# A decoder block on one core: two operand pairs made anew in the second half, rotated blocks stored one product later, and a reordered turn to the last projection

## The chip, the cores and the metric

The kernel runs on one core of a Trainium2 chip. Its engines run side by side, each through its own list of instructions in order: TensorE (PE in the profile; PEld are its weight loads), VectorE (DVE), ScalarE (ACT), GpSimd (POOL) and SyncE (SP). SP issues most of the transfers and ScalarE some stores; the rows SPq and ACTq are those issues. An engine waits on semaphores, for another engine or for a transfer, and whatever stands behind a waiting instruction on its list waits too. The metric is the device time of one execution in microseconds.

## The reference, cut to what matters

One layer of a decoder block on 2048 rows of width 1024, in float32:

```python
mod = silu(c) @ w_mod[l] + b_mod[l]
shift, scale, gate = jnp.split(mod, 3, axis=-1)
h = rms_norm(x, g_norm[l]) * (1.0 + scale[:, None, :]) + shift[:, None, :]
proj = h @ w_in[l]                       # 1024 -> 8 x 1024
x_rnn, z_rnn, q, k, v, z_attn, g_r, g_a = jnp.split(proj, IN_SPLITS, axis=-1)
xc = causal_depthwise_conv(x_rnn, conv_w[l], conv_b[l])
hr = rg_lru(xc, w_a[l], b_a[l], w_x[l], b_x[l], lam[l], positions)
y_rnn = (hr * silu(z_rnn)) @ w_out_rnn[l]
qh = apply_partial_rope(q.reshape(B, S, N_HEADS, HEAD_DIM), cos, sin)   # first 32 of 128 channels
kh = apply_partial_rope(k.reshape(B, S, N_HEADS, HEAD_DIM), cos, sin)
o = dilated_attention_mixture(qh, kh, vh)   # three (window, dilation) groups, merged by softmax weights
y_attn = (o * silu(z_attn)) @ w_out_attn[l]
merged = sigmoid(g_r + bg_r) * y_rnn + sigmoid(g_a + bg_a) * y_attn
x = x + gate[:, None, :] * (merged @ w_o[l])
return rms_norm(x, g_final)
```

## The kernel before

Every float32 product is made of three passes over rounded parts (`mm3`): high by high, high by low, low by high. So each operand is first split: ScalarE writes the rounded high part (`hi_act`, the rows of L160), and POOL or VectorE subtracts it from the raw value to get the low part (`lo_pool`, L166; `lo_dve`, L169).

The program has three stages.

*The input projection* goes over the rows in two halves of 1024 (`f` is 0, then 1). Its weights, apart from those of v, are taken in 28 pairs of column blocks, and each pair is multiplied by Strassen's scheme in Winograd's form (`strassen`): seven products in place of eight, of twelve matmuls each, with the left operands numbered 0 to 6. Three of the seven (0, 4 and 5) are plain blocks of the weight matrix (`PLAIN`), four are sums of blocks. In the first half `operand_events` loads a pair's four raw blocks (a11, a21, a22, a12; tiles R0 to R4), makes the sums s1 and s2 on VectorE, splits the seven operands into tiles S0 to S6 (`split_s`), and stores on ScalarE's queue, to sD, those that the second half will not make again. In the second half `load_next` keeps the ring of seven S tiles full: it loads an operand from sD, or, for the three plain ones of 26 of the pairs, loads the raw block, which `split_next` splits four products ahead. `prod` calls both after each product. Pairs 23 and 25 hold the first 32 channels of q's and k's heads; their results are turned by the rotary tables (`rotated`: shuffle, turn, add, and a store of four parts on SP). Pairs 22, 24, 26 and 27 are other blocks of q and k, which `plain` stores to qT and kT.

Ahead of the pairs of each half stand the products of v (`second_values` for the second half): their sums are copied out by ScalarE (tiles ev, L769) and stored by SP to vN (L771). A table `plan` says after which of their parts (t, i) the first operands of pair 0 are loaded. During the second half, pieces of other work stand at counts of products: the output projections' weights are split and stored to wD (`output_weights`), and the sums of W_o for the last stage, gated per channel, are stored to oD (`gated_weight`, tiles wo, ws).

*Attention and the output projections.* While attention runs head by head, a generator (`steps`) adds, between its products, the two projections `y_rnn` and `y_attn`: 64 tiles, each with eight steps k, with weights loaded from wD into S0 to S3 (`load_w`, `load_wd`), right operands y loaded into R0 to R3 and split (`load_y`, `split_y`; tiles yh and yl), and gates loaded to tiles fg (`load_g`, four buffers). `evict` multiplies a tile by its gate on VectorE, `store` writes it to mrT or meT. The last 16 tiles (two right operands side by side, with weights taken from the raw matrix, tiles rw) run in `output_products`, after attention.

*The last product*, `merged @ w_o`, is again by seven products: its left operands are read from meT (`operands`: raw, sums, split), its right ones F from W_o and oD (`load_o`, `gate_o`, `hi_o`, `lo_o`; tiles or, four buffers). The parts of F are numbered 0 to 27, four to a factor; `at_step` puts their loads and splits at steps of the last 16 tiles, and `late_parts` puts the last four between the last products' operands.

## Time and profile before

| | |
|---|---|
| runs shown, us | 2246.97, 2252.91, 2254.46 (median 2252.91) |
| profiled execution | 2250.71 us, span 2248.6 us |
| mean granted clock of TensorE | 0.987 |
| busy share of the span | PE 97%, PEld 82%, DVE 65%, ACT 57%, POOL 54% |
| instructions | 34354, of them 11358 matmuls |
| moved by DMA | 520.19 MB, 231 GB/s over the span |
| stores of split operands (sD) | 118 of 512 KB, 3.7 us each to landing |
| loads of split operands (sD) | 118 of 512 KB, 4.9 us |

The profile shows one execution. In a row of an engine's time line stand start and duration in microseconds, engine, source line, operation, output<-input tiles and count, and in brackets the idle time before it with what ended it. `PE X L152 <- ACT S L160: 6.8, 2, 4.4` in the table of waits says that TensorE, about to write X at line 152, waited for ScalarE's S of line 160 for 6.8 us in two waits, the longest 4.4. A row of stretches gives the length, each engine's busy time with its instructions in brackets (PE, PEld, DVE, ACT, POOL), the granted clock, the busy share of the 16 DMA engines and their GB/s.

### The profile page before, as it was taken

The numbers are of one execution on the slowest core, as the hardware profiler recorded it, in microseconds if no ns is written. First come the engines' busy times: TensorE is split into PE (matmuls) and PEld (weight loads), VectorE is DVE, ScalarE is ACT, GpSimd is POOL, SyncE is SP. The second block draws the span as 40 slices with busy tenths as digits, with TensorE's granted clock in tenths as the row PEclk, the third lists the DMA queues.
The fourth block names the chain that finished last, engine by engine and source line by source line (L and its number), as shares of the span: only waits on it lengthen the run. The fifth ranks groups of instructions, "written<-read, shape, count | busy, mean of one in ns | idle before, by whom it ended". The sixth has DMA issues, their size and how long they took to land.

```text
span 2248.6 us, 34354 instructions
## 1 busy us (share of the span) xinstructions
PE 2183.3 (97%) x11358; PEld 1847.6 (82%) x11359; DVE 1462.8 (65%) x2451; ACT 1292.7 (57%) x2560; POOL 1216.4 (54%) x903
## 2 busy tenths in 40 slices
PE   8999999999999999999999998999999999999998
PEld 5998887788877988888888887888889898977787
DVE  5578787778557664555545364467677878745776
ACT  3547767778532436766767511577677887632343
POOL 2267677677566344445445212356565656432886
PEclk9999999999999999999999999999999999999899
DMA  8354665565797647878887899989988888788553
GB/s 283 91 171 163 208 208 179 192 223 200 235 274 223 208 139 236 259 237 241 249 255 245 269 306 294 291 271 289 277 274 264 243 259 252 242 267 258 178 169 131
DMA packets 455433, 520.19 MB, mean 231 GB/s; under 512 B 90360, under 2 KB 333268, under 8 KB 454232
## 3 DMA queue, kind: packets, MB, share of 16 engines
q1 hardware_dynamic: 427492, 434.95, 63.9%
q10 hardware_dynamic: 27572, 83.00, 9.8%
q8 instruction: 90, 1.47, 0.3%
q14 instruction: 87, 0.71, 0.1%
q0 software_dynamic: 192, 0.05, 0.0%
HBM read 340.67 MB, written 177.21 MB: 230 GB/s over the span
## 4 chain that ended last, share of the span: by engine, by line
PE 53%; DMA 7%; DVE 3%; issue 2%; ACT 2%; POOL 2%; SPq 1%; ACTq 0%; POOLq 0%; DVEq 0%
PE pj L152 11%; PE X L152 9%; PE V L152 7%; PE W L152 5%; PE Z L152 5%; PE o L152 4%; PE sc L152 4%; PE Y L152 4%; PE pT L1630 1%; DMA R<-yaT 1%; PE pg L152 1%; DMA wo<-in_w_o_dram 1%; PE pT L1643 1%; DMA meT<-fg 1%; DMA oD<-s 1%
## 5 line engine op out<-in xcount | busy, mean ns | idle before, releaser
L166 POOL TENSOR_TENSOR S<-R,S 128x512 fp32r<-128x512 f32 x278 | 409.2, 1477 | 395.5 <-ACT S L160 358.4
L152 PE MATMUL X<-T,S 128*128 128x512 f32 x1344 | 330.7, 395 | 11.9 <-ACT S L160 6.8
L152 PE MATMUL V<-T,S 128*128 128x512 f32 x1344 | 325.8, 391 | 3.9 <-DVE t L468 2.7
L152 PEld LDWEIGHTS X<-T,S 128*128 128x128 f32 x1344 | 255.6, 191 | 69.0 <-ACT S L160 7.4
L152 PEld LDWEIGHTS V<-T,S 128*128 128x128 f32 x1344 | 251.0, 188 | 59.2 <-issue 1.9
L152 PE MATMUL pj<-yh,S 128*128 128x512 f32 x848 | 287.7, 397 | 5.4 <-DMA S<-wD 3.4
L160 ACT ACTIVATE S<-R 128x512 fp32r<-128x512 f32 x278 | 170.7, 622 | 129.7 <-DMA R<-in_w_in_dram 107.7
L166 POOL TENSOR_TENSOR S<-s,S 128x512 fp32r<-128x512 f32 x108 | 165.7, 1535 | 125.1 <-ACT S L160 92.8
L152 PEld LDWEIGHTS pj<-yh,S 128*128 128x128 f32 x848 | 160.9, 190 | 38.5 <-DVE fg L1861 3.8
L1546 ACT ACTIVATE pp<-pp,st 128x256 f32<-128x256 f32 (+3 forms) x256 | 133.4, 523 | 75.7 <-DVE st L1545 75.3
L152 PE MATMUL pj<-yl,S 128*128 128x512 f32 x424 | 167.8, 396 | 2.3 <-DVE yl L169 1.4
L152 PE MATMUL Y<-T,S 128*128 128x512 f32 x672 | 161.5, 389 | 0.0
L152 PE MATMUL W<-T,S 128*128 128x512 f32 x672 | 161.5, 389 | 0.0
L152 PE MATMUL Z<-T,S 128*128 128x512 f32 x672 | 161.5, 389 | 0.0
L152 PEld LDWEIGHTS Z<-T,S 128*128 128x128 f32 x672 | 126.3, 188 | 26.3
L152 PEld LDWEIGHTS W<-T,S 128*128 128x128 f32 x672 | 126.1, 188 | 26.1
L152 PEld LDWEIGHTS Y<-T,S 128*128 128x128 f32 x672 | 126.1, 188 | 26.1
L160 ACT ACTIVATE S<-s 128x512 fp32r<-128x512 f32 x108 | 67.3, 624 | 119.8 <-DVE s L292 47.6
L169 DVE TENSOR_TENSOR ptl<-pT,pth 128x384 fp32r<-128x384 f32 (+1 forms) x160 | 97.8, 628 | 49.2 <-ACT pth L160 47.0
L962 DVE SCALAR_TENSOR_TENSOR xc<-xr,par,xc 128x512 f32<-128x512 f32 x96 | 97.1, 1012 | 49.9 <-ACT xc L956 47.6
L1545 DVE CUSTOM_DVE_ANT_0 pp<-sc,msk 128x256 f32<-128x256 f32 (+3 forms) x256 | 104.2, 449 | 36.5 <-PE sc L152 34.3
L166 POOL TENSOR_TENSOR kq<-kraw,kq 128x512 fp32r<-128x512 f32 (+1 forms) x64 | 101.3, 1594 | 43.0 <-ACT kq L160 33.5
(383 smaller groups left out, 4855.4 us busy)
## 6 DMA issues: line engine op xcount, KB each, us to landing
sD<-S ACTq DMA_DIRECT2D x118, 512.0 KB, 3.7
S<-sD SPq DMA_DIRECT2D x118, 512.0 KB, 4.9
S<-wD SPq DMA_DIRECT2D x100, 512.0 KB, 5.6
R<-in_w_in_dram SPq DMA_DIRECT2D x196, 256.0 KB, 4.2
wD<-s ACTq DMA_DIRECT2D x64, 256.0 KB, 4.7
T<-in_w_mod_dram SPq DMA_DIRECT2D x8, 1024.0 KB, 12.1
vN<-ev SPq DMA_DIRECT2D x64, 128.0 KB, 2.9
zaT<-ev SPq DMA_DIRECT2D x32, 256.0 KB, 2.8
```

The source lines that it names most:

```text
L152: nc.tensor.matmul(o, lhsT=l, rhs=r, start=st, stop=sp, **kw)
L160: nc.scalar.activation(o, i, AF.Copy)
L166: nc.gpsimd.tensor_tensor(o, i, h.bitcast(F32), ALU.subtract)
L169: nc.vector.tensor_tensor(o, i, h.bitcast(F32), ALU.subtract)
L962: nc.vector.scalar_tensor_tensor(xc, xr[:, i : i + CH], cw(i), xc, ALU.mult, ALU.add)
L1545: nc.vector.tensor_tensor_reduce(pdst, s_ps, mask, 1.0, 3e38, ALU.add, ALU.min, m_)
L1546: nc.scalar.activation(pdst, pdst, AF.Exp, bias=m_, scale=-1.0, accum_out=l_)
L1630: nc.tensor.transpose(pt[:, c0 + j * P : c0 + (j + 1) * P], pp[i][:, k * P : (k + 1) * P], ident)
L1643: nc.tensor.transpose(pt[:, c * P : (c + 1) * P], pp[:, half * P : (half + 1) * P], ident)
```

## The change

TensorE's list of instructions is the same before and after. What moves is the work around it:

- Pairs 22 and 27 (`ANEW`) are not stored to sD in the first half. In the second half their seven operands are made again from four raw blocks, by the same `operand_events`. That takes away 8 stores and 8 loads of 512 KB and adds two raw block loads, eight splits, and the pairs' sums on VectorE. The remaining stores of the last pairs are emptied by a rule instead of all at the end.
- `load_next` is called again behind the work that stands after a product (`load_free`), and not while the next operand belongs to an anew pair.
- At the start of the second half, three of the first loads stand at part (6, 3) of the values' plan instead of four at (7, 0).
- `rotated` stores its block one product after the add.
- Output weights stand 4.5 products apart instead of 4.75; the groups of W_o's sums stand at 1, 13, 26 and 35 instead of 1, 10, 19 and 28, and two of the four sums are written over the loaded tile, so that the ws tile is smaller and the extra tile is gone.
- At the turn from the last head's tiles to the last 16 (tile 47, `TURN`), a weight block is loaded ahead of y's parts 5 and 6, and the gates' loads one step later. From there on the gates' loads stand one tile earlier, and every third tile uses a freed pair of yh and yl tiles in place of fg.
- Three of F's last four parts (24 to 26) are loaded into rw tiles at steps 105 to 109 and split at steps 124 to 127; only part 27 stays late.

```diff
@@ -262,9 +262,10 @@
     PLAIN = {0: (0, 0), 4: (0, 1), 5: (1, 1)}
+    ANEW = (22, 27)
     loaders, unsplit = {}, []
...
-    def operand_events(x, pieces):
+    def operand_events(x, pieces, f=0):
@@ -275,13 +276,13 @@
         def split(i, name):
+            if f:
+                assert n_loaded[0] == 7 * x + i
+                n_loaded[0] += 1
             first[7 * x + i] = t = split_s(v[name])
-            if i not in PLAIN or x not in loaders:
+            if x not in ANEW and (i not in PLAIN or x not in loaders):
                 kept.append((7 * x + i, t))
-            if len(kept) > 2:
-                k, t2 = kept.pop(0)
-                nc.scalar.dma_start(sD[k], t2[:].bitcast(F32))
-            while 7 * x + i == 28 * 7 - 1 and kept:
+            while len(kept) > 2 or kept and x >= ANEW[0] and kept[0][0] < 7 * x + i - 1:
                 k, t2 = kept.pop(0)
@@ -340,6 +341,11 @@
+    def load_free():
+        n = n_loaded
+        while n[0] - NS in used and not (n[0] < 28 * 7 and n[0] // 7 in ANEW):
+            load_next()
+
     def split_next(n):
@@ -371,7 +377,7 @@
         def take():
-            if f:
+            if f and x not in ANEW:
                 return (f, *loaded.pop(0))
@@ -385,10 +391,12 @@
                 used.add(i)
-                while n_loaded[0] - NS in used:
-                    load_next()
+                load_free()
                 split_next(i + 4)
             run_late(n_prod[0])
+            if f:
+                load_free()
+                split_next(i + 4)
@@ -457,7 +465,7 @@
             for d, fn in ((1, load), (4, split), (6, store)):
-                after_prod.setdefault(n_prod[0] + 19 * x // 4 + d, []).append(fn)
+                after_prod.setdefault(n_prod[0] + 9 * x // 2 + d, []).append(fn)
@@ -877,7 +885,8 @@
                         plan[t, i].append(lambda n=n, i=i: load_piece(n + 1, i))
-            plan[7, i].append(lambda i=i: [load_next() for _ in range(4 if i == 0 else 1)])
+            plan[7, i].append(load_next)
+        plan[6, 3].append(lambda: [load_next() for _ in range(NS - 4)])
         plan[7, 2].append(lambda: split_next(0))
@@ -1149,12 +1158,14 @@
                     nc.vector.tensor_tensor(t1[:], t1[:], t0[:], ALU.add)
+
+                def store():
                     for hh in range(4):
...
                         nc.sync.dma_start(dstT[r0 : r0 + 32, :, n * P : (n + 1) * P],
-                                          t1[hh * 32 : (hh + 1) * 32, :].rearrange("p (r j) -> p r j", r=4))
-
-                steps_after(n_prod[0], ((wait, shuffle), (wait + 1, turn), (wait + 2, add)))
+                                          v[0][hh * 32 : (hh + 1) * 32, :].rearrange("p (r j) -> p r j", r=4))
+
+                steps_after(n_prod[0], ((wait, shuffle), (wait + 1, turn), (wait + 2, add), (wait + 3, store)))
@@ -1318,25 +1329,24 @@
                 if not i:
-                    v["t"] = T(ep, [P, 3, CH], F32, "ws")
-                    v["t3"] = T(wq, [P, KH, P], F32, "s1", bufs=1)
+                    v["t"] = T(ep, [P, 2, CH], F32, "ws")
                 t = v["t"]
...
                 else:
-                    tt(v["t3"][:].rearrange("p k m -> p (k m)"), b22, b12, ALU.subtract)
-                    tt(t[:, 2, :], b21, t[:, 1, :], ALU.subtract)
+                    tt(b22, b22, b12, ALU.subtract)
+                    tt(b21, b21, t[:, 1, :], ALU.subtract)
...
             def store_sums():
-                nc.scalar.dma_start(oD[k, :, :3, :], v["t"][:])
-                nc.scalar.dma_start(oD[k, :, 3, :], v["t3"][:].rearrange("p k m -> p (k m)"))
+                nc.scalar.dma_start(oD[k, :, :2, :], v["t"][:])
+                nc.scalar.dma_start(oD[k, :, 2:, :], v[1][:])
...
-        for k, i in enumerate((1, 10, 19, 28)):
+        for k, i in enumerate((1, 13, 26, 35)):
             for d, fn in group(k):
@@ -1410,6 +1420,11 @@
             output_weights()
+            for x, (_, pieces) in enumerate(pair_order()):
+                if x in ANEW:
+                    events.extend((28 * 7 + 7 * x + d - LEAD, 15 * x + i, fn)
+                                  for i, (d, fn) in enumerate(operand_events(x, pieces, f)))
+            events.sort(key=lambda e: e[:2])
@@ -1785,7 +1800,8 @@
         tiles += [(LAST_HEAD + (i ^ (m == KT - 1)), m) for m in range(2, KT) for i in range(2)]
-        Y, G = {}, {}
+        Y, G, spare_g = {}, {}, []
+        TURN = KT * LAST_HEAD - 1
@@ -1849,8 +1865,10 @@
             G[t] = []
-            for src in (grT,) if ys is yaT else (gaT, mrT):
-                g = T(fl, [P, CH], F32, "fg", bufs=4)
+            if t == TURN + 3:
+                spare_g.extend(T(fl, [P, CH], F32, tag, bufs=NY) for tag in ("yh", "yl"))
+            for i, src in enumerate((grT,) if ys is yaT else (gaT, mrT)):
+                g = spare_g[i] if t > TURN and (t - TURN) % 3 == 0 else T(fl, [P, CH], F32, "fg", bufs=4)
                 nc.sync.dma_start(g[:], src[at_])
@@ -1875,7 +1893,8 @@
                     if u + 3 < RAW_W - 1:
-                        load_w(u + 3)
+                        if u + 3 == n_w[0]:
+                            load_w(u + 3)
                     elif u == 2 * KT * LAST_HEAD:
@@ -1884,7 +1903,7 @@
                     evict(t - 1, last)
-                if k == 3:
+                if k == (4 if t == TURN else 3) and t < TURN + 3:
                     load_g(t)
@@ -1908,9 +1927,11 @@
                         else:
-                            if k in (1, 2):
-                                load_y(j + 1, k + 4)
-                            if k == 2:
+                            if k == 1:
+                                load_y(j + 1, 5)
+                            if k == 3:
+                                load_w(n_w[0])
+                                load_y(j + 1, 6)
                                 load_y(j + 1, KT - 1)
@@ -1924,6 +1945,8 @@
                         split_y(LAST_HEAD + 1, i - (4 if i < 8 else 6))
+                    if k == KT - 1 and TURN + 2 <= t < len(tiles) - 1:
+                        load_g(t + 1)
                 yield
@@ -1965,41 +1988,49 @@
             part, k = O_PART[B_ORDER[i // KH]], i % KH
-            raw_o[i] = T(fp, [P, CH], F32, "or", bufs=4)
+            if i in range(24, 27):
+                raw_o[i] = T(fp, [P, KH, P], F32, "rw", bufs=3)[:].rearrange("p k m -> p (k m)")
+            else:
+                raw_o[i] = T(fp, [P, CH], F32, "or", bufs=4)[:]
...
         B_ORDER = "B11", "T2", "T3", "T1", "B21", "T4", "B22"
...
             if i >= 20:
-                at_step(101 + i, lambda i=i: hi_o(i))
-                at_step(102 + i, lambda i=i: lo_o(i))
-                if i > 20:
-                    at_step(103 + i, lambda i=i: load_o(i + 3))
+                at_step(100 + i, lambda i=i: hi_o(i))
+                at_step(101 + i, lambda i=i: lo_o(i))
             else:
...
                 at_step(a + 11, lambda i=i: lo_o(i))
+
+        for i in range(24, 27):
+            at_step(57 + 2 * i, lambda i=i: load_o(i))
+            at_step(65 + 2 * i, lambda i=i: gate_o(i))
+            at_step(100 + i, lambda i=i: hi_o(i))
+            at_step(101 + i, lambda i=i: lo_o(i))
+        at_step(123, lambda: load_o(27))
@@ -2052,11 +2083,8 @@
             jobs += [(7 * x + d - LEAD, len(jobs) + i, fn) for i, (d, fn) in enumerate(operands(x))]
-        late_parts = [(0, load_o, 27)]
-        for i in range(24, 28):
-            late_parts += [(d + (i - 24) // 2, fn, i) for d, fn in ((1, gate_o), (2, hi_o), (3, lo_o))]
-        for d, fn, n in late_parts:
-            jobs.append((d, len(jobs), lambda fn=fn, n=n: fn(n)))
+        for d, fn in ((2, gate_o), (3, hi_o), (4, lo_o)):
+            jobs.append((d, len(jobs), lambda fn=fn: fn(27)))
         jobs.sort(key=lambda e: e[:2])
```

ScalarE at the end of the first half (S: split operands, s: sums, sD: the store, u and T: copies out of PSUM). Before:

```order
L160 ACTIVATE S6_1164_6659<-s2_1138_6500 128x512
L283 DMA sD<-S2_1145_6552 128x1024
L286 DMA sD<-S3_1148_6578 128x1024
L286 DMA sD<-S6_1164_6659 128x1024
L401 ACTIVATE u1_1165_6665<-X_1150_6584 128x512
L537 ACTIVATE T_1153_6619<-pg_1159_6644,mod_41_235,gs_42_236 128x512
L160 ACTIVATE S0_1170_6691<-R0_1160_6649 128x512
```

and after:

```order
L160 ACTIVATE S5_1156_6621<-R3_1123_6399 128x512
L160 ACTIVATE S6_1164_6654<-s2_1138_6497 128x512
L409 ACTIVATE u1_1165_6657<-X_1150_6575 128x512
L545 ACTIVATE T_1153_6614<-pg_1159_6639,mod_41_235,gs_42_236 128x512
L160 ACTIVATE S0_1170_6683<-R0_1160_6644 128x512
L545 ACTIVATE T_1153_6614<-pg_1169_6678,mod_41_235,gs_42_236 128x512
```

The stores of pair 27's operands no longer stand between its last split (from s) and the copy u.

SP at the start of the second half (vN: stores of the values, R: raw block of S0, 4 or 5, S: loads of stored operands). Before:

```order
L771 DMA vN<-ev_1325_7802 128x2x128 x2
L771 DMA vN<-ev_1335_7941 128x2x128 x2
L771 DMA vN<-ev_1336_7945 128x2x128 x2
L255 DMA R3_1338_7950<-in_w_in_dram 128x4x128
L327 DMA S1_1339_7952<-sD 128x1024
L327 DMA S2_1340_7954<-sD 128x1024
L327 DMA S3_1341_7956<-sD 128x1024
L255 DMA R4_1343_7983<-in_w_in_dram 128x4x128
L255 DMA R0_1345_8010<-in_w_in_dram 128x4x128
L327 DMA S6_1346_8038<-sD 128x1024
```

and after:

```order
L779 DMA vN<-ev_1325_7794 128x2x128 x2
L255 DMA R3_1333_7899<-in_w_in_dram 128x4x128
L328 DMA S1_1334_7901<-sD 128x1024
L328 DMA S2_1335_7903<-sD 128x1024
L779 DMA vN<-ev_1339_7940 128x2x128 x2
L779 DMA vN<-ev_1340_7944 128x2x128 x2
L328 DMA S3_1341_7948<-sD 128x1024
L255 DMA R4_1343_7975<-in_w_in_dram 128x4x128
L255 DMA R0_1345_8002<-in_w_in_dram 128x4x128
L328 DMA S6_1346_8030<-sD 128x1024
```

The first raw block and two stored operands stand ahead of two double stores.

SP in the last tiles (meT: store of a tile, fg, yh and yl: loads of gates and of the other branch, or and rw: parts of F, R: blocks of the last product's left operand). Before:

```order
L1866 DMA meT<-fg_4034_21264 128x512
L1970 DMA or_4045_21339<-oD 128x512
L2027 DMA R2_4047_21345<-meT 128x4x128
L1854 DMA fg_4048_21356<-gaT 128x512
L1854 DMA fg_4049_21358<-mrT 128x512
L1970 DMA or_4050_21366<-oD 128x512
L2027 DMA R3_4051_21368<-meT 128x4x128
L1866 DMA meT<-fg_4040_21309 128x512
L1970 DMA or_4053_21384<-oD 128x512
```

and after:

```order
L1884 DMA meT<-yh_3961_20846 128x512
L1872 DMA fg_4041_21346<-gaT 128x512
L1872 DMA fg_4042_21348<-mrT 128x512
L1996 DMA or_4043_21351<-oD 128x512
L1999 DMA rw_4045_21357<-in_w_o_dram 128x512
L2058 DMA R2_4046_21359<-meT 128x4x128
L1999 DMA rw_4047_21368<-in_w_o_dram 128x512
L1996 DMA or_4048_21378<-oD 128x512
L1999 DMA rw_4049_21380<-in_w_o_dram 128x512
L2058 DMA R3_4050_21382<-meT 128x4x128
L1884 DMA meT<-fg_4034_21300 128x512
```

The parts of F that came last are loaded between R2 and R3 into rw, and the gates of a tile stand before the blocks R2 and R3 instead of between and behind them.

10 lines of the change are left out of this document (5 added, 5 removed).

## The prediction

> **What bounds the kernel now.** I read the page first, for the busy shares, then the stretches around the waits, then the engines' own rows there. TensorE is busy 97% of the span, so only the rest can be won.
>
> ```profile
> span 2248.6 us, 34354 instructions
> PE 2183.3 (97%) x11358; PEld 1847.6 (82%) x11359; DVE 1462.8 (65%) x2451; ACT 1292.7 (57%) x2560; POOL 1216.4 (54%) x903
> ```
>
> The table of TensorE's waits (total, times, longest) names who ended them:
>
> ```profile
> PE X L152 <- ACT S L160: 6.8, 2, 4.4
> PE X L152 <- POOL S L166: 4.9, 2, 4.2
> PE Z L152 <- ACT S L160: 4.7, 1, 4.7
> PE pg L527 <- DVE t L547: 3.9, 1, 3.9
> PE pj L152 <- DMA S<-wD: 3.4, 1, 3.4
> PE pj L152 <- ACT yh L160: 2.1, 1, 2.1
> PE pj L152 <- DVE yl L169: 1.4, 2, 1.2
> ```
>
> A wait costs more than its length, because the granted clock falls behind it. Seven stretches, from the view by stretch (length, then each engine's busy time, the clock, the DMA share, GB/s), hold the waits that the change can reach; I call them G, A, B, C, D, E, F in order of time:
>
> ```profile
> 710.00:724.00 14.00, 10.08 (x38) 7.92 (x37) 6.12 (x8) 4.78 (x8) 7.69 (x7) 0.76 0.90 279
> 826.00:841.00 15.00, 10.45 (x47) 8.32 (x46) 1.10 (x2) 3.34 (x7) 1.28 (x1) 0.77 0.81 250
> 1352.00:1363.00 11.00, 7.95 (x27) 5.76 (x26) 2.74 (x6) 1.75 (x3) 2.56 (x3) 0.84 1.04 328
> 1399.00:1411.00 12.00, 8.53 (x29) 6.05 (x28) 5.66 (x9) 3.98 (x7) 0.00 (x0) 0.86 1.02 339
> 1981.00:2002.00 21.00, 16.82 (x62) 11.98 (x61) 6.65 (x9) 5.29 (x9) 6.42 (x5) 0.92 0.89 285
> 2073.00:2087.00 14.00, 9.30 (x30) 7.15 (x29) 8.56 (x12) 5.27 (x10) 9.76 (x7) 0.76 0.83 241
> 2095.00:2110.00 15.00, 9.87 (x31) 6.94 (x31) 12.27 (x13) 6.37 (x14) 12.38 (x8) 0.77 0.42 138
> ```
>
> The loss of a stretch is its length less TensorE's busy time, plus one minus the clock, times its length. G: 3.9 + 0.24 x 14 = 7.3 us. A: 4.55 + 3.45 = 8.0. B: 3.05 + 1.76 = 4.8. C: 3.47 + 1.68 = 5.2. D: 4.18 + 1.68 = 5.9. E: 4.7 + 3.36 = 8.1. F: 5.13 + 3.45 = 8.6. Together 47.9 us, the most that the change can bring here; TensorE's own order of instructions is the same in both kernels, so nothing can come from it.
>
> **The change part by part.** G, end of the first half. ScalarE (ACT, ACTq for its DMA issues) holds the copy u1 behind the last two stores of pair 27's operands:
>
> ```profile
> 712.01 4.25 ACTq L286 DMA_DIRECT2D sD<-S  x2
> 716.31 0.60 ACT L401 ACTIVATE u<-X 128x512 f32<-128x512 f32 x1 [5.80 <-DMA sD<-S]
> 717.61 0.81 DVE L547 TENSOR_SCALAR t<-pg,gs,mod 128x512 f32<-128x512 f32 x1
> 711.19 4.83 SPq L474 DMA_DIRECT2D R<-in_w_in_dram  x4
> ```
>
> VectorE makes t only behind u, and TensorE waits 3.9 us for it. Pair 27 is no longer stored, so u1 follows its split at once, 5.8 us sooner. What is late next are the loads issued from 711.19, which the following products split; I leave 1.0 us for them. Gain 6.3 of 7.3.
>
> A, start of the second half. S0 is split from a raw block whose load stands on SP behind eight stores of values, and the last four of those wait for ScalarE's copies at 827:
>
> ```profile
> 811.35 18.21 SPq L771 DMA_DIRECT2D vN<-ev  x8
> 827.46 0.59 ACT L769 ACTIVATE ev<-X 128x512 f32<-128x512 f32 x1
> 829.65 0.46 SPq L255 DMA_DIRECT2D R<-in_w_in_dram  x1
> 833.13 0.63 ACT L160 ACTIVATE S<-R 128x512 fp32r<-128x512 f32 x1 [5.09 <-DMA R<-in_w_in_dram]
> L166 POOL TENSOR_TENSOR S<-R,S 128x512 fp32r<-128x512 f32 x278 | 409.2, 1477 | 395.5 <-ACT S L160 358.4
> ```
>
> Now R, S1 and S2 are issued ahead of the last four stores, with eight earlier ones behind them no more, so R lands while the copies run. The split follows the copy that ends at 828.05: 0.63 us for the high part, 1.48 for the low one on POOL, done at 830.2. Now the high part alone ends at 833.8. The 4.4 us of wait in the table shrink to 0.8 or so, too little to bring the clock down. Gain 7.0 of 8.0. S3, still behind the stores, is due three products later.
>
> B and C, end of the second half. SP runs behind, held by stores that wait for their adds and by two wo loads:
>
> ```profile
> 1345.90 2.52 SPq L1154 DMA_DIRECT2D qT<-t  x4
> 1350.42 1.48 SPq L255 DMA_DIRECT2D R<-in_w_in_dram  x2
> 1356.24 0.63 ACT L160 ACTIVATE S<-R 128x512 fp32r<-128x512 f32 x1 [17.37 <-DMA R<-in_w_in_dram]
> 1351.67 2.88 PE L152 MATMUL Y<-T,S 128*128 128x512 f32 x12
> 1396.04 0.93 SPq L361 DMA_DIRECT2D R<-yaT  x2
> ```
>
> A four-part store takes 2.5 us of SP, 0.63 an issue. Between the previous pair's S0 load and the R issued at 1350.42 stand 24 issues instead of 30, and a rotated block's store comes one product behind its add, so that SP no longer stands still for it. Six issues are 3.8 us: R lands near 1352.4, not 1356.24, its low part is done 2.1 us later, at 1354.5, and the product is due when Y's twelve matmuls from 1351.67 end, at 1354.4. Gain 4.0 of 4.8: 0.1 of wait and what SP's later lateness may put back. In C the R loads of 1396.04 move ahead of kT stores, and pair 27's four 512 KB loads are gone; VectorE's low part (1.2 us of wait above) stays, with the rest of the clock. Gain 3.5 of 5.2.
>
> What pairs 22 and 27 cost instead: seven splits from four raw blocks each, where there were three splits and four loads of stored operands. Eight more splits are 8 x 0.63 = 5 us of ScalarE and 8 x 1.48 = 12 us of POOL, in a part of the program where POOL has room:
>
> ```profile
> 1236.00:1300.00 64.00, 64.00 (x286) 52.95 (x285) 25.86 (x35) 31.38 (x46) 16.83 (x13) 1.00 0.88 286
> 1296.58 2.88 PE L152 MATMUL X<-T,S 128*128 128x512 f32 x12
> 1299.30 2.88 PE L152 MATMUL V<-T,S 128*128 128x512 f32 x12
> ```
>
> POOL is busy 16.8 of 64 us there, and a product takes 2.72 (1296.58 to 1299.30) against POOL's 1.48. If that cover is gone, each of the two pairs starts late as in A, by 8.0 us; between 0 and 16 I take 2, near the end that POOL's row speaks for. The first half loses eight stores of 512 KB on ScalarE's queue, which G shows blocking; I count no gain beyond G. Storing oD's sums from wo itself, and output weights 4.5 instead of 4.75 products apart, move no end of the path: nothing, unless ScalarE's queue blocks as in G (up to 7.3).
>
> D, the turn to the last projection. TensorE waits 3.4 us for a wD block issued late:
>
> ```profile
> 1978.73 0.49 SPq L355 DMA_DIRECT2D S<-wD  x1
> ```
>
> It goes ahead of one R and two fg loads: three issues and a store's, about 2 us of the 3.4. But no byte is saved, the R that it passes now lands behind its 512 KB, and the loads of y's last parts, each waiting for the split before it, bound the same tiles. Ends 0 and 5.9; I take 2.0, nearer the lower, as the DMA share is 0.89.
>
> E and F, the last tiles. With four fg buffers SP waits for a store to land before each pair of loads; VectorE, in order, waits for the loads, and the sums of the first last-stage operand stand behind it. In F it waits the same way for an or load:
>
> ```profile
> 2066.40 0.93 SPq L1854 DMA_DIRECT2D fg<-gaT  x1
> 2072.74 0.69 DVE L1859 TENSOR_TENSOR fg<-pj,fg 128x512 f32<-128x512 f32 x1 [4.62 <-DMA fg<-gaT]
> 2075.01 0.68 DVE L2038 TENSOR_TENSOR s<-R,R 128x512 f32<-128x512 f32 x1
> 2089.35 0.42 SPq L1973 DMA_DIRECT2D or<-in_w_o_dram  x1
> 2096.25 0.69 DVE L1978 TENSOR_TENSOR or<-or,gate_b 128x512 f32<-128x512 f32 x1 [4.97 <-DMA or<-in_w_o_dram]
> ```
>
> Every third tile now uses freed yh and yl buffers, fg is loaded a tile (two products, 5.4 us) ahead, and three of the four last or loads move before the sums, their splits too. 4.6 us of VectorE's wait in E and 5.0 in F are what TensorE waits (4.7 and 4.2). I leave 1.1 and 1.6 us for POOL, whose low parts are next: 7.0 and 7.0.
>
> Sum: 6.3 + 7.0 + 4.0 + 3.5 + 2.0 + 7.0 + 7.0 = 36.8, less 2 is 34.8. The profiled execution took 2250.71 us (2.1 outside the span), 2.2 under the median of 2252.91; 2250.7 - 34.8 + 2.2 = 2218.
>
> [...] A kept wait need not stay as cheap as it is. This one let the clock be, though B's, not longer, halved it:
>
> ```profile
> 633.11 3.04 PE L152 MATMUL X<-T,S 128*128 128x512 f32 x12 [3.52 <-ACT u L401]
> ```
>
> [...]
>
> **Rivals.** First, the tail is bound by its transfers: DMA shares of 0.89 and 0.83 in D and E speak for it, the 0.42 in F against it. Then D, E and F keep their waits: 2250.7 - 20.8 + 2 + 2.2 = 2234.
>
> Second, slower: SP is held by the raw blocks made anew. Pair 22's fourth load needs a buffer that POOL frees only when it has split the first one, and behind it on SP stand the S loads of pairs 23 to 26 and 27's blocks. They are due from 1296.58 on, five products (13.6 us) behind that split; for it speaks that SP already runs late (1350.42 above), against it POOL's room. If the hold passes 13.6 us, five pairs start as A does: 5 x 8.0 = 40 us, more than the 34.8, so 2258.
>
> Third, the change does not do what it says: the waits only pass on to what is late next, as a DMA issue on SP or ScalarE that waits for another transfer (5.8 us in G). For it: every stretch but F has the DMA at 0.8 or more. 2250.
>
> **How the numbers follow.** The sum 0.57; tail bound by transfers 0.20; hold on SP 0.13; passed on 0.10. The likeliest gives 2218, its own range 2204 (all 47.9 won: 2250.7 - 47.9 + 2.2 = 2205) to 2230. The whole range goes to 2248, which leaves out the slower case and part of the third. About 0.3% (6.8 us) is what a measurement can tell from no change: faster 0.79 (sum, tail rival, a fifth of the third), same 0.07, slower 0.14.
>
> **What would show it.** Right: no store of S between the last split and u1 on ScalarE; the R of the second half issued before 825; SP's R of 1350 and 1396 some 4 us sooner; VectorE's waits for fg and or near 2073 and 2096 gone; clock 0.99 and over. Wrong: TensorE waiting for S at pairs 22 to 27 between 1260 and 1400, or for F and S at 2070 to 2110 still.

## The result, and the profile after

The changed kernel takes 2226.69 us (median of 4 runs, 2225.20 to 2229.14) against 2252.19 us for the kernel before beside it (2246.97 to 2254.46, 4 runs): a ratio of 0.9902 with a 95% interval of 0.9888 to 0.9916. 25.5 us were won where 34.8 were forecast; 2226.7 lies inside the whole range and inside the likeliest case's own, 8.7 us above the forecast of 2218.

The page of the changed kernel, its first rows (busy time, share of the span, instructions):

```profile
span 2227.2 us, 34367 instructions
PE 2174.6 (98%) x11359; PEld 1843.2 (83%) x11359; DVE 1480.7 (66%) x2459; ACT 1297.4 (58%) x2568; POOL 1233.6 (55%) x911
```

and six rows of its table of TensorE's waits (total, times, longest):

```profile
PE V L152 <- DVE t L476: 7.5, 5, 3.0
PE pj L152 <- DVE yl L169: 7.2, 1, 7.2
...
PE pj L152 <- ACT yh L160: 2.2, 2, 1.4
...
PE W L152 <- DVE fg L1877: 2.1, 1, 2.1
PE pj L152 <- POOL yl L166: 1.7, 2, 0.9
...
PE Z L152 <- DVE yh L1877: 1.3, 1, 1.3
```

The waits for S of before (6.8, 4.9 and 4.7 us) are gone from the table, all but a few tenths, and so are the 3.9 for t behind u and the 3.4 for wD. In their place stands one wait that before had no counterpart, 7.2 us for yl, and the waits of V for t (a result that VectorE copies out of PSUM with a sum) have grown from 2.7 to 7.5 us.

Since TensorE's instructions are the same ones, each matmul can be set against itself: its start after, less its start before. Where that difference changes, time was won (negative) or lost. The rows are in us, the times those of the trace before; the last column is a second profile of the changed kernel, beside other runs.

| place | times before | forecast | after | after again |
|---|---|---|---|---|
| pair 22's stores, not in the forecast | 629 to 633 | 0 | -3.8 | -3.8 |
| G, end of the first half | 714 to 724 | -6.3 | -6.5 | -6.5 |
| A, start of the second half | 829 to 840 | -7.0 | -7.1 | -7.2 |
| B | 1354 to 1362 | -4.0 | -5.1 | -5.1 |
| behind B, waits for t | 1362 to 1382 | 0 | +3.2 | +1.4 |
| C | 1397 to 1423 | -3.5 | +10.1 | +8.8 |
| D, the turn | 1981 to 2000 | -2.0 | -1.4 | -1.5 |
| E | 2075 to 2089 | -7.0 | -2.1 | -2.9 |
| F | 2089 to 2110 | -7.0 | -8.2 | -8.1 |
| sum | | -36.8 | -20.9 | -24.9 |

The 2 us that the forecast takes off for the start of the two pairs have no row of their own. The two spans differ by 21.4 us (2248.6 less 2227.2), so the first column of measured numbers accounts for them. Other places, among them 381, 400, 1474, move by up to 1.8 us to either side and not alike in every profile; I read nothing into them.

The same in the view by stretch of the changed kernel (length, busy time of PE, PEld, DVE, ACT, POOL, the clock, the DMA share, GB/s), at the times at which it now does that work, as it runs up to 25 us ahead: G and A, then what became of C, D, and E:

```profile
704.00:713.00 9.00, 9.00 (x47) 7.44 (x46) 5.79 (x9) 5.46 (x10) 7.26 (x6) 1.00 0.84 240
814.00:823.00 9.00, 8.73 (x52) 7.49 (x51) 1.29 (x2) 3.32 (x6) 1.29 (x1) 1.00 0.52 142
...
1375.00:1411.00 36.00, 24.05 (x91) 17.78 (x89) 14.46 (x24) 9.14 (x16) 5.82 (x6) 0.86 0.98 331
1972.00:1990.00 18.00, 15.21 (x55) 10.82 (x53) 6.02 (x8) 5.68 (x9) 6.58 (x5) 0.91 0.94 310
2056.00:2076.00 20.00, 16.59 (x66) 12.95 (x65) 17.68 (x19) 8.21 (x15) 13.05 (x8) 0.91 0.84 236
```

The first has no gap left, the second one of 0.27 us, and both have the full clock: nearly all that could be won there is won. The 36 us of the third hold 12 us of idle TensorE, and there the forecast failed.

**What happens in C.** Row by row, from the time line of the changed kernel (start, duration, engine, line, operation, and in brackets the idle time before it and what ended it):

```profile
1355.82 0.68 DVE L1339 TENSOR_TENSOR wo<-wo,wo 128x512 f32<-128x512 f32 x1
1356.42 0.69 DVE L1340 TENSOR_TENSOR wo<-wo,ws 128x512 f32<-128x512 f32 x1
...
1358.25 0.68 DVE L301 TENSOR_TENSOR R<-R,R 128x512 f32<-128x512 f32 x1
...
1358.98 0.93 SPq L255 DMA_DIRECT2D R<-in_w_in_dram  x2
...
1359.96 6.37 SPq L1165 DMA_DIRECT2D kT<-t  x8
...
1366.43 3.95 SPq L1195 DMA_DIRECT2D kT<-t  x4
...
1370.71 0.83 SPq L1325 DMA_DIRECT2D wo<-in_w_o_dram  x2
...
1375.60 1.23 DVE L1328 TENSOR_TENSOR wo<-wo,gb 128x1024 f32<-128x1024 f32 x1 [7.54 <-DMA wo<-in_w_o_dram]
...
1379.22 4.36 PE L152 MATMUL V<-T,S 128*128 128x512 f32 x12 [3.02 <-DVE t L476]
...
1381.85 0.33 ACTq L1344 DMA_DIRECT2D oD<-wo  x1
...
1382.26 1.69 SPq L367 DMA_DIRECT2D R<-yaT  x2
...
1391.16 0.63 ACT L160 ACTIVATE yh<-R 128x512 fp32r<-128x512 f32 x1 [6.88 <-DMA oD<-wo]
1391.32 1.29 DVE L169 TENSOR_TENSOR yl<-R,yh 128x512 fp32r<-128x512 f32 x2 [7.01 <-DMA oD<-wo]
...
1392.06 0.79 PE L152 MATMUL pj<-yl,S 128*128 128x512 f32 x1 [7.23 <-DVE yl L169]
```

and the two longest of SP's waits between 1335 and 1400:

```profile
SPq L255 <- DVE R L301: 11.5, 1, 11.5
SPq L1195 <- DMA T<-yaT: 4.3, 1, 4.3
```

The 11.5 us are SP standing before pair 27's fourth raw block: its buffer comes free only when VectorE's difference at L301 has read the first one, and that one follows the sums of W_o's third group (L1339, L1340). Behind the hold SP issues twelve kT stores, and only then the two wo loads of the last group, at 1370.71. VectorE sits 7.54 us for them, with the sum t that TensorE waits for behind them (3.02). The group's store to oD is issued at 1381.85. The rows at 1391.16 and 1391.32 show the next stage's splits waiting until that store has landed, 9.3 us after its issue; that yh and yl lie in the memory of wo and ws is read from the built kernel's addresses. TensorE waits 7.23 us. So the last group, which now stands at 35 instead of 28, ends inside the turn to the next stage, and SP's hold makes it later still. The last R loads from yaT do move ahead of two kT stores, as the forecast's step on C has it, but they are issued 7.9 us later than before against TensorE's matmuls (at 1382.26 here, 1396.04 before, in a kernel that was 21.7 us ahead until this place).

**Behind B.** The same queue of VectorE explains the 3.2 us lost right behind B. From 1342.56, when W_o's third group gets its load (5.78 us of wait for it), VectorE works almost without a pause until 1362.9: that group's gating and sums, the rotated block, and pair 27's own sums (L292, L293, L301, 0.7 us each). TensorE waits 0.63 and 2.09 us for a t that stands among them. This is read from the rows; no run varies it alone. The first row and the longer wait:

```profile
1342.56 1.40 DVE L1328 TENSOR_TENSOR wo<-wo,gb 128x1024 f32<-128x1024 f32 x1 [5.78 <-DMA wo<-in_w_o_dram]
...
1359.58 3.01 PE L152 MATMUL V<-T,S 128*128 128x512 f32 x12 [2.09 <-DVE t L476]
```

### The profile page after: what moved, and what is told of

Read it like the earlier page. It is cut to its first block, busy times and chain, and to the rows that moved or that the text cites. A ratio compares the mean times of both kernels' runs of the same rounds, so it can differ in the third digit from the quotient of the medians.

```text
span 2227.2 us, 34367 instructions
## 1 busy us (share of the span) xinstructions
PE 2174.6 (98%) x11359; PEld 1843.2 (83%) x11359; DVE 1480.7 (66%) x2459; ACT 1297.4 (58%) x2568; POOL 1233.6 (55%) x911
## 4 chain that ended last, share of the span: by engine, by line
PE 53%; DMA 6%; DVE 5%; issue 3%; ACT 2%; SPq 2%; POOL 2%; ACTq 0%; DVEq 0%; POOLq 0%
PE pj L152 10%; PE X L152 9%; PE V L152 8%; PE W L152 6%; PE Z L152 6%; PE Y L152 4%; PE o L152 4%; PE sc L152 4%; DMA R<-in_w_in_dram 1%; PE pT L1645 1%; PE pg L152 1%; DMA R<-oT 1%; PE pT L1658 1%; POOL kq L166 1%; DMA kT<-t 1%
## 5 line engine op out<-in xcount | busy, mean ns | idle before, releaser
L166 POOL TENSOR_TENSOR S<-R,S 128x512 fp32r<-128x512 f32 x280 | 414.6, 1486 | 364.6 <-ACT S L160 324.8
L152 PE MATMUL X<-T,S 128*128 128x512 f32 x1344 | 323.6, 389 | 0.3 <-POOL S L166 0.3
L166 POOL TENSOR_TENSOR S<-s,S 128x512 fp32r<-128x512 f32 x114 | 174.0, 1526 | 124.7 <-ACT S L160 80.5
```

Of the source, the lines that this page charges most:

```text
L152: nc.tensor.matmul(o, lhsT=l, rhs=r, start=st, stop=sp, **kw)
L166: nc.gpsimd.tensor_tensor(o, i, h.bitcast(F32), ALU.subtract)
```

## The experiments

Each edit is made to the changed kernel. Medians stand beside the kernel before on the same chip; the comparisons by place are with the changed kernel's first trace unless another is named, positive for time lost.

**W_o's groups where they were.**

```diff
-        for k, i in enumerate((1, 13, 26, 35)):
+        for k, i in enumerate((1, 10, 19, 28)):
```

> The changed kernel with one thing undone: the four groups of W_o's sums stand at 1, 10, 19 and 28 again, not at 1, 13, 26 and 35. Theory L (the late last group is the cause of the 10.0 us lost between 1376 and 1411): its wo loads, VectorE's gating and the store of oD, on whose memory the projection's first yh and yl wait, come early again; the waits of 3.0 and 7.2 us go, and the time falls from 2226.7 by 9 to 12, to about 2216. Theory H (SP held for 11.5 us by pair 27's fourth raw block is the cause): the kT stores and what stands behind them stay late; it falls by under 4, to 2223 or more.

2223.16 us against 2245.11; ratio 0.9906 (0.9889 to 0.9922), no different from the changed kernel's. 1345 to 1411 gets 3.9 us shorter than in the changed kernel's first trace and 0.8 than in its second. The wait of 7.2 us for yl is gone, as theory L has it, but not the 9 to 12 us that it promised: what remains are three waits for yh (6.4 us), and the hold on SP is still 8.8.

**The fourth raw block of an anew pair two products later.**

```diff
-        yield -1, lambda: raw("a12", 0, 1)
+        if not f:
+            yield -1, lambda: raw("a12", 0, 1)
...
+        if f:
+            yield 1, lambda: raw("a12", 0, 1)
```

> The changed kernel, with the fourth raw block (a12) of the two pairs made anew in the second half loaded two products later, behind the split of a11 that frees its buffer. The groups of W_o stay at 1, 13, 26 and 35. Theory H: SP no longer stands still for 11.5 us at pair 27 and 5.4 at pair 22, the last wo load goes out some 8 us sooner, and the waits at 1376 and 1384 fall by 8 or more: about 2218. Theory L: the last group still stands at the end and the store of oD still lands late; under 4 us are won, 2223 or more. If a12 now comes too late for its own split, a new wait of up to 5 us at pair 27's fifth operand takes it back.

2227.31 us against 2245.11; ratio 0.9916 (0.9902 to 0.9931). Only 1345 to 1360 gets shorter, by 1.3 us; against the second trace even that is gone. The edit shortens SP's hold at pair 27 from 11.5 to 7.3 us and does not remove it. With the last group still at 35, TensorE waits 5.9 us for yl, whose split again ends its wait with the landing of the oD store, and 8.0 us for yh, whose split waits for T from yaT. A shorter hold alone is worth nothing that a run can tell.

**Both together.** The two edits above in one kernel.

> Both at once: groups of W_o at 1, 10, 19 and 28, and a12 of the anew pairs two products later. If L and H each carry a part, this is faster than either alone: 2213 or so. If L carries all, it equals the run with the old groups within 2 us; if H carries all, it equals the run with a12 later.

2220.32 us against 2245.11; ratio 0.9887 (0.9872 to 0.9901). That is 2.8 and 7.0 us below the two runs before it, which ran beside it, and the four executions of each do not overlap; the 2213 expected if each cause carries a part is not reached. Against the changed kernel's first trace 1345 to 1411 gets about 9 us shorter, against its second about 6, more than the two alone (3.9 and 1.1, or 0.8 and a loss). The longest of SP's waits of this kernel between 1315 and 1400, then TensorE's from 1330 to 1420:

```profile
SPq L255 <- DVE R L302: 4.8, 1, 4.8
```

```profile
PE V L152 <- ACT S L160: 1.9, 1, 1.9
PE pj L152 <- ACT yh L160: 1.6, 1, 1.6
PE pj L152 <- DVE yl L169: 1.4, 2, 1.2
PE V L152 <- DVE t L479: 0.7, 1, 0.7
```

One profile alone swings by some us here, so I set all of them side by side: from 1362 to 1425, in the times of before, the seven profiles that make both pairs anew and leave both edits out lose 9.2 to 13.3 us against before; the old groups alone lose 9.4, the later block alone 11.8; the three kernels with both lose 4.2, 6.0 and 7.6. So neither edit alone shows a gain outside the swing, and both together do: each cause hides behind the other. Yet against the kernel before, B and C together come out at -1.0 us (-5.1 and +4.1), not at the -7.5 of the forecast. The rest, some 6 us, is five short waits and the clock (0.95 on average from 1340 to 1405 of the kernel with both edits). No run takes apart whether writing two sums over wo, the wider spacing of the output weights, or the anew pair's own splits hold them. That stays open.

**Only pair 27 made anew; pair 22 stored again.**

```diff
-    ANEW = (22, 27)
+    ANEW = (27,)
```

> Only pair 27 is made anew; pair 22's operands are stored in the first half and loaded in the second, as before. Theory S (the 3.5 us wait at 629, which the prediction did not count, went because pair 22's four stores of 512 KB no longer stand in the transfers at 590 to 612): the wait for u at 629 comes back, 3 to 5 us, while the gain at 714 (6.5 us) stays, as that comes from pair 27. Rival: the wait at 629 hangs on which transfer happens to share a semaphore with a store, and is gone or back whatever pair 22 does; it stays away here. In the second half SP's wait at pair 22 (5.4 us) goes, which costs TensorE nothing now, so nothing is won by it.

2227.96 us in one run, against 2245.11. G stays won, with pair 27 still not stored; no run stores pair 27 again, so G's cause rests on the rows. The wait near 630, which the changed kernel no longer has, is back: 4.0 us long, and 5.8 us are lost at that place. ScalarE there, in this kernel and then in the changed one (`sD<-S`: a store of an operand; u: the copy out of PSUM that TensorE needs):

```profile
630.36 0.33 ACTq L287 DMA_DIRECT2D sD<-S  x1
630.73 0.60 ACT L409 ACTIVATE u<-X 128x512 f32<-128x512 f32 x1 [5.11 <-DMA R<-in_w_in_dram]
```

```profile
627.45 0.33 ACTq L287 DMA_DIRECT2D sD<-S  x1
627.83 0.60 ACT L409 ACTIVATE u<-X 128x512 f32<-128x512 f32 x1 [4.64 <-DMA R<-in_w_in_dram]
```

The hold on ScalarE's queue is there in both (5.11 and 4.64 us; 5.26 before), and ends when a raw block lands. What pair 22's missing stores do is let that block's load go out earlier, and u comes 4.7 us sooner against TensorE's matmuls (2.9 by the rows, in a kernel that is 1.8 us behind there). The four 512 KB stores of pair 22 stood at 599 to 612 before. That the loss comes back with them is shown, though the edit also moves the point from which the remaining stores are emptied by the rule; that they act through SP's issue of R is read from the trace and was not varied.

**The plan at the start of the second half as it was.**

```diff
-            plan[7, i].append(load_next)
-        plan[6, 3].append(lambda: [load_next() for _ in range(NS - 4)])
+            plan[7, i].append(lambda i=i: [load_next() for _ in range(4 if i == 0 else 1)])
```

> The changed kernel with the start of the second half as before: the first four operands of pair 0 are loaded at part (7, 0) of the values' plan, behind the last two double stores of v. If the order on SP is what won 7.1 us there, the wait of 4.4 us at pair 0's first product and the half clock behind it come back: 6.5 to 8 us lost there, nothing elsewhere. Rival: the win came from stores or transfers of the first half that are gone; then it stays won, and under 2 us change.

2232.77 us in one run; the kernel before, run once beside this one and the next three, took 2243.30. A loses 8.6 us, a little more than the 6.5 to 8 expected, and the wait that ends it is S's again:

```profile
PE X L152 <- ACT S L160: 5.9, 1, 5.9
```

A is this edit alone, and its whole gain.

**The turn's loads as they were** (no weight block ahead of y's parts, the gates a step earlier).

```diff
-                if k == (4 if t == TURN else 3) and t < TURN + 3:
+                if k == 3 and t < TURN + 3:
...
-                            if k == 1:
-                                load_y(j + 1, 5)
-                            if k == 3:
-                                load_w(n_w[0])
-                                load_y(j + 1, 6)
+                            if k in (1, 2):
+                                load_y(j + 1, k + 4)
+                            if k == 2:
                                 load_y(j + 1, KT - 1)
```

> The changed kernel with the turn to the last projection as before (y's parts 5 and 6 ahead of the third weight block, gates one step earlier). The turn won 1.4 us of the 7.4 lost there. If the order only passes the wait from the weight block to y's part 5 and F's parts, bound by transfers, this run loses 0 to 3 us there, and the wait for the weight block (3.4 us) is back in place of the waits for yl and F. If instead the new order is what costs the remaining 6, this run is no slower at all.

2226.86 us in one run. D loses 1.9 us, against a gain there of 0.5 to 2.0 in the profiles that keep the edit. TensorE's waits from 1960 to 2000, in this kernel and in the changed one:

```profile
PE pj L152 <- DMA S<-wD: 3.7, 1, 3.7
```

```profile
PE pj L152 <- ACT yh L160: 1.4, 1, 1.4
PE pj L152 <- POOL yl L166: 0.9, 1, 0.9
```

The change swaps one wait of 3.7 us for two, 2.3 us in all, as the step on D had it: the weight block passes y's parts, and these are late next.

**The gates' loads and their tiles as before the change** (four fg buffers, loads within the tile).

```diff
-            if t == TURN + 3:
-                spare_g.extend(T(fl, [P, CH], F32, tag, bufs=NY) for tag in ("yh", "yl"))
...
-                g = spare_g[i] if t > TURN and (t - TURN) % 3 == 0 else T(fl, [P, CH], F32, "fg", bufs=4)
+                g = T(fl, [P, CH], F32, "fg", bufs=4)
...
-                if k == (4 if t == TURN else 3) and t < TURN + 3:
+                if k == (4 if t == TURN else 3):
...
-                    if k == KT - 1 and TURN + 2 <= t < len(tiles) - 1:
-                        load_g(t + 1)
```

> The changed kernel with the gates' loads of the last 16 tiles as before: four fg buffers alone, loaded in the tile itself; F's parts 24 to 26 stay early in rw. E (about 2075 before) won about 4 us. If the gates' loads held it, SP waits again for stores to land, and E loses 4 us or more, up to the 7.6 of before, as parts 24 to 26 now stand in the same queue. Rival: F's early parts won E; then this run changes by under 1.5 us.

2231.34 us in one run; 2064 to 2076 loses 2.8 us, between the two expectations. One wait of 5.1 us for S stands where the changed kernel has 1.3 and 2.1. How far this can be read: in the kernel with only pair 27 anew, where nothing is edited in the tail, the same place is 2.3 us shorter than in the changed kernel's first profile. The loss stands outside the swing all the same: E wins 1.4 to 4.4 us against before in every profile that leaves the tail as changed, and loses 0.8 here.

**F's last parts as before the change** (parts 24 to 27 loaded into or tiles after the sums).

```diff
-            if i in range(24, 27):
-                raw_o[i] = T(fp, [P, KH, P], F32, "rw", bufs=3)[:].rearrange("p k m -> p (k m)")
...
-        for i in range(24, 27):
-            at_step(57 + 2 * i, lambda i=i: load_o(i))
-            at_step(65 + 2 * i, lambda i=i: gate_o(i))
...
+        late_parts = [(0, load_o, 27)]
+        for i in range(24, 28):
+            late_parts += [(d + (i - 24) // 2, fn, i) for d, fn in ((1, gate_o), (2, hi_o), (3, lo_o))]
```

> The changed kernel with F's parts 24 to 27 as before, loaded and gated late into or buffers; gates' loads stay early. F (about 2100 before, 8.2 us lost) comes back if the late or load held VectorE there: 6 to 8 us lost at the first product of the second operand. E gets better by up to 3 us, since VectorE's gates of 24 to 26 (5.4 us of wait for the rw load at 2051 after) no longer stand ahead of the tile's evict. Rival: with the gates' loads early the queue is short enough that the or load comes in time; under 2 us lost.

2224.52 us in one run. F loses 6.5 us, as the forecast's step on F says, but E wins 5.6, so that it stands 7.6 us better than before the change: net, this edit is worth 1 us. Here are the same two stretches without it, the second with the loss in it:

```profile
2050.00:2066.00 16.00, 16.00 (x72) 13.24 (x72) 12.94 (x13) 6.66 (x12) 11.54 (x8) 1.00 0.96 304
2066.00:2090.00 24.00, 19.69 (x79) 15.04 (x78) 18.93 (x24) 10.81 (x22) 20.49 (x14) 0.93 0.48 160
```

With the edit TensorE loses time in the first stretch instead. VectorE, in the changed kernel:

```profile
2056.61 0.69 DVE L2004 TENSOR_TENSOR rw<-rw,gate_b 128x512 f32<-128x512 f32 x1 [5.39 <-DMA rw<-in_w_o_dram]
2058.19 0.69 DVE L2004 TENSOR_TENSOR rw<-rw,gate_b 128x512 f32<-128x512 f32 x1 [0.89 <-DMA rw<-in_w_o_dram]
2058.80 0.68 DVE L1877 TENSOR_TENSOR fg<-pj,fg 128x512 f32<-128x512 f32 x1
...
2066.40 1.78 DVE L169 TENSOR_TENSOR F<-or,F 128x512 fp32r<-128x512 f32 x1
2068.11 1.76 DVE L169 TENSOR_TENSOR F<-rw,F 128x512 fp32r<-128x512 f32 x1
2069.79 0.68 DVE L1877 TENSOR_TENSOR fg<-W,fg 128x512 f32<-128x512 f32 x1
```

The part's gate product waits 5.39 us for its load, with an output tile's eviction and the operand's sums behind it, and the part's split stands ahead of the eviction for which TensorE waits 2.1 us. Two readings were left: the wait for the load does the harm, or VectorE has too much to do in these 20 us (17.68 busy, in the view by stretch above). The next runs tell them apart.

**The changed kernel again**, beside the next three runs.

> The changed kernel again, beside the other three. Every theory: the ratio to the kernel before stays near 0.990 (0.9888 to 0.9916 was the interval), and the same places lose as in its first trace: 8 to 12 us at 1360 to 1411 against the first promise of a gain, 3 to 5 us in the tail at 2063 to 2076.

2224.69 us against 2246.24; ratio 0.9897 (0.9874 to 0.9920). The places are in the table at the top: C is lost again, B is won again, and the loss behind B varies by some 2 us from one profile to the next.

**The two edits of C, and the three gate products behind the sums.**

```diff
-            at_step(65 + 2 * i, lambda i=i: gate_o(i))
+            at_step(97 + i, lambda i=i: gate_o(i))
```

> The groups of W_o's sums at 1, 10, 19, 28, pair 27's and 22's fourth block two products later, and the gate products of F's parts 24 to 26 placed behind the sums of the first last-stage operand instead of ahead of an output tile's eviction. Theory T (what is left of the loss in the tail is VectorE's eviction standing behind a gate product that waits 5.4 us for its load): TensorE's waits of 1.3 and 2.1 us at 2063 to 2071 and the halved clock behind them go, 3 to 5.5 us, and the parts of F, still loaded early, keep what was won at 2083 to 2110; with 9 to 10 us at 1345 to 1411 it ends 12 to 15 us below the changed kernel, ratio 0.984 to 0.986. Rival (VectorE is simply full there, 12 of 14 us, and the three gate products only change places with the splits): under 1.5 us in the tail, 9 to 11 below in all, ratio 0.9865 to 0.989.

2219.73 us against 2246.24; ratio 0.9874 (0.9846 to 0.9903), 5 us below the changed kernel beside it, with intervals that overlap and executions that do not (2217.18 to 2222.26, 2222.88 to 2225.81). Theory T wanted 12 to 15, its rival 9 to 11. The gain is C's; in the tail nothing is won (1.1 us lost against the changed kernel's second trace). No gate product waits for its load any more, the sums start 3.8 us sooner (2048.03 after 2060.73, in a kernel that is 8.9 us ahead there), and TensorE waits as long as it did. Its waits from 2040 to 2110:

```profile
PE W L152 <- DVE fg L1880: 2.5, 1, 2.5
PE Z L152 <- ACT F L160: 1.2, 1, 1.2
```

3.7 us, after 3.4. So theory T is wrong: the wait for the load goes, and the loss stays. The rival is what is left. VectorE is busy 19.75 us from 2048 to 2068 here, and its work has only changed places; that its fullness is the bound is argued from this, not varied.

**The same, two steps later still.**

```diff
-            at_step(65 + 2 * i, lambda i=i: gate_o(i))
+            at_step(99 + i, lambda i=i: gate_o(i))
```

> As the one before, with the three gate products two steps later still, so that the second and third stand behind the next eviction (yh from Z). Theory T: no difference of more than 1 us either way, since that eviction has to wait for Z's product anyway. Rival (full VectorE): each gate product of 0.7 us that stands ahead of an eviction costs its own length, so this one is 1 to 2 us faster than the one before.

2221.20 us against 2246.24; ratio 0.9882 (0.9860 to 0.9904). One wait, of 3.9 us, takes the place of the two. The eviction of Z's tile is freed, the next one pays for it: the sum is the same. The gain of 1 to 2 us that the rival expected of this run did not come, so its price of an eviction's delay is not borne out.

**The rotated blocks stored with the add again.**

```diff
-                steps_after(n_prod[0], ((wait, shuffle), (wait + 1, turn), (wait + 2, add), (wait + 3, store)))
+                steps_after(n_prod[0], ((wait, shuffle), (wait + 1, turn), (wait + 2, add), (wait + 2, store)))
```

> The changed kernel, with the rotated blocks stored right behind their add again. By the prediction's step on B the later store is what lets SP go on: SP's raw block loads at 1335 to 1357 come 2 to 4 us later, and TensorE loses 1 to 4 us at 1340 to 1411. Rival (SP is held there by pair 27's fourth block, which waits for its buffer, and the store's place decides nothing): under 1 us in TensorE's offset at 1340 to 1411, and the total within 2 us of the changed kernel.

2224.08 us in one run, 0.6 below the changed kernel's median beside it; its span is 0.1 us shorter than that of the second profile of the changed kernel. Between 1340 and 1411 the offset changes by 0.6 to 1.1 us against that profile, to the better, and B's own gain is 5.1 us as with the later store. The rival holds in that the store's place decides nothing here.

## Why the prediction was right, and where it was not

The likeliest case came in: G, A and D right in mechanism and near in size, B and F right in mechanism and about 1 us too small, E too large by 4 to 5, C wrong in sign.

G (6.3 forecast, 6.5 measured) and A (7.0 and 7.1, and 8.6 when its one edit is undone) came out by the rows quoted for them, though the closeness of G's number is in part luck. The step left 1.0 us of 7.3 for loads that would be late next; none is late, no gap is left, and still 6.5 were won. So the bound of 7.3 was itself too high: it takes the clock's share of the idle time as well (0.24 of 14 us; of the 10.08 busy ones it is 2.4, and the sum 6.3). In A the step left 0.8 us of wait and took it as too little to bring the clock down: 0.27 us is left, at a clock of 1.00, and in the trace before the clock is 1.00 behind waits of 0.74, 0.60 and 0.76 us too (at 423, 591 and 702). In D the block ahead of y's parts was worth 1.4 of the 2.0, and what was named as late next, the splits of y's last parts, is what remains.

B was right about where TensorE waited: the wait for S is gone, and 5.1 us are won in every profile, against 4.0. What swings is the wait for t right behind it, 3.2 and 1.4 us in two profiles of the same kernel, which no term held. One reason given for B was wrong: the store one product behind its add lets nothing go that was held. Which of the other edits lets R out earlier was not varied.

C is the step that failed: "Storing oD's sums from wo itself, and output weights 4.5 instead of 4.75 products apart, move no end of the path: nothing", and with it the 3.5 us of gain for pair 27's missing loads. I counted the instructions of W_o's groups and not where the last one stands: seven products later, with a store at its end out of memory that the next stage's first splits write. The exception that the step made, ScalarE's queue blocking as in G, is not what happened: the memory of the store was held, not the queue. Putting the groups back alone wins nothing outside the swing of the place; together with a shorter hold on SP it wins about 9 us (6 by the second profile). The hold was the second rival, and its mechanism is there, 5.4 us at pair 22 and 11.5 at pair 27 (released by VectorE's difference, not by POOL's split), but priced at the wrong pair: at 22 the rows of SP between 1240 and 1300 show it, and TensorE waits for no operand there; at 27, where SP was late already, it delays the loads of W_o's group. It reached none of the 40 us given to it. The 2 us set down for both pairs' start stand in no row as such. The clock behind a wait can fall either way, as the forecast has it. In the trace before it stays at 1.00 behind 3.52 us at 633, and is granted 0.50 from 1359 to 1361, behind B's 2.37 and 0.68 us. In the first profile of the changed kernel the 2.1 us before W's product at 2071 have 0.50 behind them from 2071.6 to 2075, and the 3.02 us in C have 4.36 us for twelve matmuls behind them, where 2.88 is usual. What makes the difference no run shows; the length of the wait alone does not. What mattered was which waits came.

E and F: 14.0 forecast, 10.2 and 11.1 measured. The step put 7.0 on each, as if they were apart, and each is right without the other: F won 8.2, and E would have won 7.6 without F's edit. With it E won 2.1 and 2.9. Undoing the gates' edit costs 2.8, undoing F's edit 1.0 (6.5 lost in F, 5.6 won in E): F's work was moved into E's stretch, where VectorE was the engine that TensorE waits for in the first profile. The row to read was VectorE's busy time after the move, 17.7 of 20 us, where I left time for POOL alone.

The 3.8 us near 630 were in no term ("I count no gain beyond G"). The wait's row was quoted in the forecast, though only for the clock. The eight missing stores were counted as room on a queue, without asking at which wait four of them stand. That these 3.8 us came as a gain is luck: without them the result would be 2230.5, just outside the likeliest case's own range.

## What to carry to other kernels

When a piece of work is moved later, look up what uses its memory next: a store counts until it lands, 9 us after its issue here, not until it is issued. When work is moved out of one gap into another place, add it to the busy time of the engine that TensorE waits for at that place; a gap can move with it, and the two edits' gains do not add up. A queue's hold costs what is late behind it (TensorE waited for nothing behind the 5.4 us at pair 22, and the 11.5 at pair 27 delayed W_o's loads): ask at each place that it touches, and not at the first alone.

## What the runs showed of the hardware

VectorE's gate product of 128x512 took 0.68 us at 2044.79, while POOL rested, and 1.78 us at 2046.72, beside POOL's low part. Two rows of VectorE in the changed kernel, without and beside POOL, and one whose first input lies in PSUM, then POOL's rows at the second and the third:

```profile
2044.79 0.68 DVE L2004 TENSOR_TENSOR or<-or,gate_b 128x512 f32<-128x512 f32 x1
...
2046.72 1.78 DVE L2004 TENSOR_TENSOR or<-or,gate_b 128x512 f32<-128x512 f32 x1
...
2064.71 0.68 DVE L1877 TENSOR_TENSOR yh<-Z,yh 128x512 f32<-128x512 f32 x1
```

```profile
2046.22 1.73 POOL L166 TENSOR_TENSOR F<-or,F 128x512 fp32r<-128x512 f32 x1 [2.50 <-ACT F L160]
...
2064.20 3.43 POOL L166 TENSOR_TENSOR F<-or,F 128x512 fp32r<-128x512 f32 x2
```

The instruction that reads Z out of PSUM keeps its 0.68 us beside POOL's two. In E, F's three low parts on VectorE, at 2063.42, 2066.40 and 2068.11, took 1.36, 1.78 and 1.76 us beside POOL's. That POOL's work is the cause is read from these rows; no run moved it away to measure it.

A store on ScalarE's queue waited for a load on SP's: the waits in the rows at 627 and 630 end with the landing of R, 4.6 and 5.1 us after ScalarE's last work, though the store does not use R. In the trace ScalarE's queue waits, just before the store, for the semaphore that this store counts on. In the kernel before it is the one on which an R load of SP had been counted last; the load landed at 632.01, and the store went out at 632.09. That this is the cause is read off, and was not varied.
